# The first layer's last three modulations: VectorE products with row sums in place of plain TensorE matmuls

## The chip, the cores and the metric

The kernel runs on one core of a Trainium2 chip. The metric is the device time of one execution in microseconds (us). Engines are named as the profile names them: PE is TensorE (PEld its weight loads), DVE is VectorE, ACT is ScalarE, POOL is GpSimd, and SP is SyncE, whose queue issues nearly all DMAs of this kernel.

## The reference, cut to what matters

Two layers of a diffusion backbone over 256 context and 256 latent tokens of width 1024. Each layer is a half-step SwiGLU, four token mixers side by side on one normalised input (an S5 recurrence, a latent attention MLA, an HGRN2 recurrence and a grouped attention GQA), merged by gates, and a second half-step SwiGLU. Every sub-layer is modulated by shift, scale and gate vectors that come from the conditioning:

```
mod_lat = (jax.nn.silu(c) @ w_ada[layer] + b_ada[layer]).reshape(b, 1, N_MOD, D_MODEL)
mod_ctx = (jax.nn.silu(c_ctx) @ w_ada[layer] + b_ada[layer]).reshape(1, 1, N_MOD, D_MODEL)
```

So there are nine modulations a layer, each a product of two vectors (latent and context) with a 1024 x 1024 matrix of weights, 4 MB. Numbers 6, 7 and 8 are the shift, scale and gate of the second SwiGLU; they are needed only at the end of the mixing stage and after it.

## The kernel before

The activations stand transposed, 128 channels to a partition block and 512 tokens along the row. Every large product is written as three fp32r matmuls on a high and a low part of both operands (`mm3`, lines 345 to 347). A weight piece is 128 x 1024: `piece` (line 323) loads it through the SP queue into one of three buffers (`wraw`, tile `raw`), ACT casts the high part (L317, `whi`) and DVE subtracts for the low part (L318, `wlo`).

The program is `begin`, `ffn(0,0)`, `mix(0)`, `ffn(0,1)`, `ffn(1,0)`, `mix(1)`, `ffn(1,1)`. In `mix`, generators stand for the pieces of work. `lane` (line 1649) steps through tracks of attention or recurrence work, and after each step `fill` adds a share of projection and merge matmuls ("fillers", tiles `pj`, `pk`, `br`) that keep PE busy, and `next(self.slow)` takes one step of a slow side job, here the modulations. The slow job starts with the GQA track (line 1722) and has 24 steps. In layer 0 the second plan entry, `h|GM`, runs the second HGRN half (`h`) beside GQA and then MLA (`G`, `M`).

The text is recorded in this order, and a scheduler then gives each engine a fixed sequence of its own, which the engine works through in order; between engines only semaphores decide. The attention's unit (`attend`, line 836) is a chain over three engines: score matmul `s` (PE, L841), row maximum and its negation (DVE, L843 and L844), exponential `e` (ACT, L846), reciprocal and scaling (DVE, L847 and L848), transposes `pt` (PE, L853), a copy `p` (DVE L858 or ACT L856), and the product with the values `od` (PE, L868). The HGRN half has similar chains: `ckd`, `cqd` and `cx` between DVE (L1088, L1090, L1127 to L1133) and ACT, `ckt`, `cst`, `clv` and `cdg` on PE.

There are two ways to compute a modulation. `ada_pe` (line 434) does it on PE: for each of 8 pieces of 128 input rows (tile `araw`, in the same three `wraw` buffers) four plain fp32 matmuls with the two vectors as a 32-column stationary operand, into one PSUM bank of tag `f` that is held for all 8 steps, then one DVE copy (`adaev`, L448) and two PE transposes (`adat`, L451):

```
for q in range(4):
    nc.tensor.matmul(ps[32 * q : 32 * q + 32, :256], self.cS[:, kb], raw[:, 256 * q : 256 * q + 256], ...)
```

`ada` (line 401) does it on DVE from a transposed copy of the weights (`w_adaT`, output channels on partitions): for each half of the inputs (`kh`) it loads the two vectors spread over all partitions (`cr`, L411), applies Silu on ACT (L412), and for each of 4 pieces a modulation does four products with a row sum (L424), each over 128 x 512. It is the way the other modulations are done (0,2 to 0,5 beside the first SwiGLU; all of layer 1 beside SwiGLUs):

```
w = raw[:, 512 * i : 512 * i + 512]
for v in range(2):
    nc.vector.scalar_tensor_tensor(w if v else junk, w, 1.0, S[v], op0=ALU.mult, op1=ALU.mult,
                                   accum_out=t[:, 2 * op + i, v : v + 1])
```

`modulation` (line 457) adds the bias and the norm weights in either case.

Of the kernel before, what the change touches and what calls it, by code (L numbers as in the profile page):

```python
# [27 lines left out]
ALL_T = (0, NTOK)  # L28
# [158 lines left out]
class Kern:  # L187
# [295 lines left out]
    def begin(self, lag=1, first=1, spread=3, early=0):  # L483
# [4 lines left out]
        m = self.mod[0][:2] = [self.cpool.tile([P, KB, 2], F32, name=f"mod0_{j}") for j in range(2)]  # L488
        H, ws, banks = self.new_h(), [], []

# [42 lines left out]
        for t in range(KB + lag):  # L533
# [7 lines left out]
            for half in hv:  # L541
                p, q = half[1]
                self.pre_block(0, 0, ob, H, half, rs[:, p:q])
            if first <= ob < first + 4:
# [3 lines left out]
            for i, w in enumerate(ws):  # L548
                for kb in range(ob + 1) if i == ob - first else (ob,):
                    c = slice(kb * P, kb * P + P)  # L550
                    self.mm3(banks[i], (w[0][:, c], w[1][:, c]), H[kb], kb == 0, kb == KB - 1)
            mark, tc.cur_priority = tc.cur_priority, now
        tc.cur_priority = mark
        return H, banks

    def pre_block(self, l, s, kb, H, half, rs):

        nc = self.nc
        v, (a, b) = half
        sh, sc = self.mod[l][3 * s], self.mod[l][3 * s + 1]  # L560
        hh, hl = H[kb]
        t = self.u("ht")
        nc.vector.scalar_tensor_tensor(
            t[:, a:b], self.x[kb][:, a:b], sc[:, kb, v : v + 1], rs, op0=ALU.mult, op1=ALU.mult)
        nc.scalar.activation(hh[:, a:b], t[:, a:b], AF.Identity, bias=sh[:, kb, v : v + 1])  # L565
        nc.vector.scalar_tensor_tensor(
            hl[:, a:b], t[:, a:b], sh[:, kb, v : v + 1], hh[:, a:b].bitcast(F32), op0=ALU.add, op1=ALU.subtract)
# [1198 lines left out]
    def run(self):  # L1766
        nc = self.nc
        self.setup()
        self.opt = [
            dict(plan=('H', 'h|GM', 'S'), rates=(1.5, 0.4, 1, 1, 1), share=0.75, pk='f', pv='a', pq='a', vtt='a', us='a', s1='f', sD='f', cap=18, gap=1),  # L1770
            dict(plan=('H', 'h', 'G', 'M', 'S'), rates=(1.7, 1.3, 1.5, 1.5, 0.8), share=0, pk='a', pv='a', pq='a', vtt='f', us='a', s1='f', sD='f', cap=12, gap=2),
        ]

        H, banks = self.begin()
        self.gpre += self.vectors("norm_pre", 24, [1])
        self.gpost = self.vectors("norm_post", 24, range(DEPTH))
        self.mvec = self.vectors("mvec", 8, range(DEPTH))
        self.beside = [[self.ada(0, range(2, 6), False), 0.6, 0], [self.behind(self.s5_tables(0)), 0.6, 0]]
        W = self.A["ffn"]
        head = lambda l: [self.A["win"][l, i] for i in FIRST]  # L1780
        H = self.ffn(0, 0, ALL_T, H, (0, 1), head(0), banks)
        self.finish()
        self.lower_bounds()
        H = self.mix(0, ALL_T, H, (0, 2), (x for j in range(6, 9) for x in self.ada_pe(0, j)), [W[1, i] for i in range(self.start)])
        self.beside = [[self.behind(self.s5_tables(1)), 0.6, 0], [self.behind(self.ada(1, range(3), False)), 0.6, 0]]
        H = self.ffn(0, 1, ALL_T, H, (1, 0), [W[2, i] for i in range(self.start)])
        self.finish()
        self.beside = [[self.behind(self.ada(1, range(3, 9))), 0.9, 0]]
        H = self.ffn(1, 0, ALL_T, H, (1, 1), head(1))
        self.finish()  # L1790
        H = self.mix(1, LAT_T, H, (1, 2), iter(()), [W[3, i] for i in range(4)])
        self.ffn(1, 1, LAT_T, H, None)
        for kb in range(KB):
            nc.sync.dma_start(self.out[kb * P : (kb + 1) * P, :], self.x[kb][:, NCTX:])
# [23 lines left out]
```

## Time and profile before

| | |
|---|---|
| median of 3 runs | 2426.26 us (2425.04 to 2430.54) |
| the profiled execution: its own time | 2430.84 us |
| its span, first to last instruction | 2429.1 us, mean granted TensorE clock 0.972 |
| PE busy | 2278.5 us, 94% of the span |
| PEld busy | 1923.3 us, 79% |
| DVE busy | 1641.2 us, 68% |
| ACT busy | 902.7 us, 37% |
| POOL busy | 166.4 us, 7% |
| DMA | 326.84 MB, mean 135 GB/s |

Times in the rows are in us from the start of the span unless marked ns. A busy time is the time in which at least one instruction of the engine runs. An instruction's duration and the spacing to the next one differ, since neighbours overlap. What an engine does on the average of the span says little here: the change touches one stretch, and what bounds that stretch has to be read there.

### The profile page before, as it was taken

How to read it: one execution, taken by the hardware profiler on the slowest of the kernel's cores; microseconds unless marked ns; L12 is line 12 of the kernel's file. 1: busy time of each engine (PE TensorE's matmuls, PEld its weight loads, DVE VectorE, ACT ScalarE, POOL GpSimd, SP SyncE). 2: the span in 40 equal slices, each digit the busy share in tenths (PEclk: the TensorE clock that was granted, in tenths of full speed). 3: DMA queues.
4: the chain of work that ended last, by engine and by line, in shares of the span. 5: the costliest groups of instructions: out<-in, count | busy, mean ns of one | idle time of the engine just before them, and what ended most of it. 6: DMA issues, size and time to landing. Idle time of an engine off the chain costs nothing.

```text
span 2429.1 us, 39327 instructions
## 1 busy us (share of the span) xinstructions
PE 2278.5 (94%) x15428; PEld 1923.3 (79%) x15428; DVE 1641.2 (68%) x3929; ACT 902.7 (37%) x1551; POOL 166.4 (7%) x144
## 2 busy tenths in 40 slices
PE   7969989999999999988799999999998999998997
PEld 4757878987667777887677898888898887898997
DVE  5876566766565565799665558868757787678554
ACT  3313323363443323442222233323234664345443
POOL 0093000000000000006510000000000000000000
PEclk9989999999999999999899999999998999998999
DMA  7526454232441242233454423656542332354663
GB/s 237 180 90 183 155 170 156 73 94 77 132 161 41 86 150 83 79 122 120 149 166 158 135 86 117 204 177 196 173 139 81 109 109 69 122 187 134 186 184 114
DMA packets 111226, 326.84 MB, mean 135 GB/s; under 512 B 16256, under 2 KB 23168, under 8 KB 111040
## 3 DMA queue, kind: packets, MB, share of 16 engines
q1 hardware_dynamic: 109024, 320.65, 42.8%
q10 hardware_dynamic: 2016, 3.67, 0.5%
q8 instruction: 121, 1.98, 0.3%
q14 instruction: 65, 0.53, 0.1%
HBM read 311.20 MB, written 15.17 MB: 134 GB/s over the span
## 4 chain that ended last, share of the span: by engine, by line
PE 73%; DVE 14%; DMA 6%; ACT 3%; issue 2%; POOL 2%; SPq 0%; DVEq 0%; ACTq 0%; POOLq 0%
PE h L345 8%; PE h L347 8%; PE h L346 8%; PE y L345 5%; PE y L347 5%; PE y L346 5%; PE pj L345 5%; PE pj L347 5%; PE pj L346 5%; DMA araw<-in_w_adaT_dram 3%; DVE wlo L318 3%; DVE aj L424 2%; DMA raw<-in_ffn_dram 2%; PE s L841 2%; DVE araw L424 1%
## 5 line engine op out<-in xcount | busy, mean ns | idle before, releaser
L317 ACT CAST whi<-raw 128x1024 fp32r<-128x1024 f32 x402 | 421.1, 1050 | 843.0 <-DMA raw<-in_ffn_dram 308.8
L318 DVE TENSOR_TENSOR wlo<-raw,whi 128x1024 fp32r<-128x1024 f32 x402 | 499.5, 1245 | 302.9 <-ACT whi L317 300.3
L347 PE MATMUL h<-hh,wlo 128*128 128x512 f32 (+1 forms) x1472 | 529.8, 361 | 22.1 <-DVE wlo L318 22.1
L345 PE MATMUL h<-hh,whi 128*128 128x512 f32 (+1 forms) x1472 | 531.2, 362 | 16.8 <-DVE gf L686 11.2
L346 PE MATMUL h<-hl,whi 128*128 128x512 f32 (+1 forms) x1472 | 528.3, 360 | 0.0
L347 PEld LDWEIGHTS h<-hh,wlo 128*128 128x128 f32 x1472 | 283.4, 193 | 67.7 <-DVE wlo L318 24.7
L345 PEld LDWEIGHTS h<-hh,whi 128*128 128x128 f32 x1472 | 284.1, 193 | 62.0 <-issue 12.1
L346 PEld LDWEIGHTS h<-hl,whi 128*128 128x128 f32 x1472 | 284.0, 193 | 39.2
L345 PE MATMUL y<-gh,whi 128*128 128x256 f32 (+1 forms) x902 | 290.3, 322 | 2.6 <-ACT t L685 2.6
L347 PE MATMUL y<-gh,wlo 128*128 128x256 f32 (+1 forms) x902 | 290.8, 323 | 0.0
L346 PE MATMUL y<-gl,whi 128*128 128x256 f32 (+1 forms) x902 | 290.5, 322 | 0.0
L345 PE MATMUL pj<-hh,whi 128*128 128x256 f32 (+1 forms) x800 | 276.5, 348 | 3.3 <-ACT hh L565 2.7
L347 PE MATMUL pj<-hh,wlo 128*128 128x256 f32 (+1 forms) x800 | 274.5, 345 | 3.5 <-DVE wlo L318 3.5
L346 PE MATMUL pj<-hl,whi 128*128 128x256 f32 (+1 forms) x800 | 275.4, 346 | 0.0
L345 PEld LDWEIGHTS y<-gh,whi 128*128 128x128 f32 x902 | 171.7, 190 | 15.7 <-ACT t L685 2.8
L346 PEld LDWEIGHTS y<-gl,whi 128*128 128x128 f32 x902 | 171.7, 190 | 13.0
L347 PEld LDWEIGHTS y<-gh,wlo 128*128 128x128 f32 x902 | 171.7, 190 | 12.8
L345 PEld LDWEIGHTS pj<-hh,whi 128*128 128x128 f32 x800 | 154.1, 194 | 23.6 <-issue 5.2
L347 PEld LDWEIGHTS pj<-hh,wlo 128*128 128x128 f32 x800 | 153.9, 193 | 23.6 <-DVE wlo L318 4.8
L346 PEld LDWEIGHTS pj<-hl,whi 128*128 128x128 f32 x800 | 154.2, 193 | 18.4 <-issue 3.9
L424 DVE SCALAR_TENSOR_TENSOR aj<-araw,cr 128x512 f32<-128x512 f32 x112 | 89.8, 802 | 81.8 <-DMA araw<-in_w_adaT_dram 80.1
L687 ACT CAST gh<-gf 128x512 fp32r<-128x512 f32 (+1 forms) x88 | 49.8, 565 | 161.4 <-DVE gf L686 160.0
(391 smaller groups left out, 3188.3 us busy)
## 6 DMA issues: line engine op xcount, KB each, us to landing
raw<-in_ffn_dram SPq DMA_DIRECT2D x267, 512.0 KB, 3.8
araw<-in_w_adaT_dram SPq DMA_DIRECT2D x104, 512.0 KB, 4.1
raw<-in_win_dram SPq DMA_DIRECT2D x102, 512.0 KB, 3.7
araw<-in_w_ada_dram SPq DMA_DIRECT2D x24, 512.0 KB, 4.0
raw<-in_wout_dram SPq DMA_DIRECT2D x17, 512.0 KB, 3.5
raw<-in_wbr_dram SPq DMA_DIRECT2D x16, 512.0 KB, 3.7
araw<-in_w_ada_dram SPq DMA_DIRECT2D x22, 256.0 KB, 5.9
s5G<-s5g SPq DMA_DIRECT2D x16, 256.0 KB, 4.5
```

Source lines behind the costliest of these rows:

```text
L317: self.nc.scalar.copy(hi, src)
L318: self.nc.vector.tensor_tensor(lo, src, hi.bitcast(F32), op=ALU.subtract)
L345: mm(ps, wh, xh, start=start, stop=False, skip_group_check=True)
L346: mm(ps, wh, xl, start=False, stop=False, skip_group_check=True)
L347: mm(ps, wl, xh, start=False, stop=stop, skip_group_check=True)
L424: nc.vector.scalar_tensor_tensor(w if v else junk, w, 1.0, S[v], op0=ALU.mult, op1=ALU.mult, accum_out=t[:, 2 * op + i, v : v + 1])
L687: nc.scalar.copy(gh[:, a:b], gf[:, a:b])
L841: nc.tensor.matmul(s[:, :w], q[:, j * P : (j + 1) * P], k[:, :w], start=True, stop=True)
```

## The change

In `mix(0)` the slow side job is another generator:

```diff
-        H = self.mix(0, ALL_T, H, (0, 2), (x for j in range(6, 9) for x in self.ada_pe(0, j)), [W[1, i] for i in range(self.start)])
+        H = self.mix(0, ALL_T, H, (0, 2), self.ada(0, range(6, 9), False), [W[1, i] for i in range(self.start)])
```

With `banks` False the Silu results stay in SBUF (`cr` is overwritten in place). Both generators have 24 steps and load 24 pieces of 512 KB through the SP queue. `ada_pe` finishes one modulation after another; `ada` does the first half of the inputs for all three, then the second half, so that modulation 6 is ready after step 16.

The fixed sequences of three engines, at three places. In the names, the part behind the underscore is a running number.

DVE, one GQA unit in the middle of the stretch, from its row maximum to its scaled exponentials. Before:

```order
L843 TENSOR_REDUCE m_5716<-s_5714 128x1
L1107 SCALAR_TENSOR_TENSOR cst_5576<-cst_5576,et_5638,cst_5693 128x64
L844 TENSOR_SCALAR m_5716<-m_5716 128x1
L318 TENSOR_TENSOR wlo_5766<-raw_5763,whi_5765 128x1024
L1107 SCALAR_TENSOR_TENSOR cst_5576<-cst_5576,et_5638,cst_5693 128x64
L847 RECIPROCAL m_5716<-m_5716 128x1
L1127 TENSOR_TENSOR cx_5735<-cw_5591 128x512
L848 TENSOR_SCALAR e_5719<-e_5719,m_5716 128x256
```

The same unit in the changed kernel, with a few rows ahead of it:

```order
L1107 SCALAR_TENSOR_TENSOR cst_5576<-cst_5576,et_5647,cst_5702 128x64
L424 SCALAR_TENSOR_TENSOR araw_5712,mod_6_5631<-araw_5712,cr_5637 128x512
L424 SCALAR_TENSOR_TENSOR aj_5640,mod_6_5631<-araw_5712,cr_5634 128x512
L843 TENSOR_REDUCE m_5725<-s_5723 128x1
L424 SCALAR_TENSOR_TENSOR araw_5712,mod_6_5631<-araw_5712,cr_5637 128x512
L844 TENSOR_SCALAR m_5725<-m_5725 128x1
L424 SCALAR_TENSOR_TENSOR aj_5640,mod_7_5632<-araw_5732,cr_5634 128x512
L424 SCALAR_TENSOR_TENSOR araw_5732,mod_7_5632<-araw_5732,cr_5637 128x512
L424 SCALAR_TENSOR_TENSOR aj_5640,mod_7_5632<-araw_5732,cr_5634 128x512
L847 RECIPROCAL m_5725<-m_5725 128x1
L1127 TENSOR_TENSOR cx_5744<-cw_5591 128x512
L848 TENSOR_SCALAR e_5728<-e_5728,m_5725 128x256
```

The products stand between the unit's own steps; the next units look alike, until all 96 are done.

PE, the scores of the unit before that and what follows. Before:

```order
L853 MATMUL pt_5658<-cst,e_5601 128x128 x2
L841 MATMUL s_5663<-dq_5077,dq_4801 128x256
L442 MATMUL adaps_5631<-araw_5703,cS 32x256 x3
L347 MATMUL pj_5613<-hh_3591,wlo_5610 128x512
L345 MATMUL pj_5613<-hh_3593,whi_5609 128x512
L442 MATMUL adaps_5631<-araw_5723,cS 32x256
L1095 MATMUL ckt_5687<-cst,ckd_5640 128x128 x2
L442 MATMUL adaps_5631<-araw_5723,cS 32x256 x3
L346 MATMUL pj_5613<-hl_3594,whi_5609 128x512
L347 MATMUL pj_5613<-hh_3593,wlo_5610 128x512
L1095 MATMUL ckt_5687<-cst,ckd_5640 128x128
L1100 MATMUL cst_5693<-vc_4311,ckt_5688 64x64 x2
```

In the changed kernel:

```order
L347 MATMUL pj_5613<-hh_3593,wlo_5610 128x512
L853 MATMUL pt_5667<-cst,e_5601 128x128 x2
L841 MATMUL s_5672<-dq_5077,dq_4801 128x256
L1095 MATMUL ckt_5696<-cst,ckd_5649 128x128 x3
L1100 MATMUL cst_5702<-vc_4311,ckt_5697 64x64 x2
L853 MATMUL pt_5718<-cst,e_5677 128x128 x2
L841 MATMUL s_5723<-dq_5077,dq_4801 128x256
```

The modulation matmuls are gone and nothing has moved into their place. From the first of these score matmuls to the twelfth, PE has 120 projection matmuls before and 110 in the changed kernel; four of the ten stand ahead of the first one now, the rest behind the twelfth.

ACT, ahead of the first of these units' exponentials. Before:

```order
L1086 ACTIVATE et_5638<-cw_5591 128x1
L1087 ACTIVATE ckd_5640<-cw_5591 128x128
L1086 ACTIVATE et_5638<-cw_5591 128x1
L1087 ACTIVATE ckd_5640<-cw_5591 128x128
L1086 ACTIVATE et_5638<-cw_5591 128x1
L1087 ACTIVATE ckd_5640<-cw_5591 128x128
L1089 ACTIVATE cqd_5639<-cw_5591 128x512
L846 ACTIVATE e_5668,m_5665<-s_5663,m_5665 128x256
```

In the changed kernel:

```order
L1086 ACTIVATE et_5647<-cw_5591 128x1 x3
L412 ACT_TABLE_LOAD
L412 ACTIVATE cr_5634<-cr_5634 128x512
L412 ACTIVATE cr_5637<-cr_5637 128x512
L1087 ACT_TABLE_LOAD
L1087 ACTIVATE ckd_5649<-cw_5591 128x128 x3
L1089 ACTIVATE cqd_5648<-cw_5591 128x512
L846 ACTIVATE e_5677,m_5674<-s_5672,m_5674 128x256
```

Two Silu and two table loads stand ahead of the exponentials now. The same four instructions stand a second time in the middle of the stretch, for the second half of the inputs.

## Rows read from the trace of the kernel before

**Rows 1.** The page, part 1: busy time (share of span) and instructions by engine.

```profile
PE 2278.5 (94%) x15428; PEld 1923.3 (79%) x15428; DVE 1641.2 (68%) x3929; ACT 902.7 (37%) x1551; POOL 166.4 (7%) x144
```

**Rows 2.** Busy time by stretch: PE, PEld, DVE, ACT, POOL (instructions), clock, DMA share, GB/s.

```profile
629.87:715.10 85.23, 81.26 (x801) 47.99 (x801) 53.41 (x157) 35.06 (x82) 1.36 (x3) 0.96 0.52 168
720.00:1000.00 280.00, 274.20 (x1836) 213.24 (x1835) 164.72 (x309) 97.25 (x175) 0.45 (x4) 0.99 0.29 90
```

**Rows 3.** Chain of work that ended last, 600 to 760 us, by line.

```profile
by line: PE pj L345 15.9%; PE pj L347 14.8%; PE pj L346 14.0%; PE adaps L442 9.7%; PE s L841 8.0%; PE od L868 5.2%; PE cdg L1174 4.7%; PE pt L853 4.5%; PE hs L787 3.4%; PE oc L1192 2.9%; DMA araw<-in_w_ada_dram 2.5%; PE hb L810 2.1%; PE oc 
```

**Rows 4.** Line 442, all its matmuls (duration ns min/median/max, first and last start).

```profile
L442 PE MATMUL adaps<-araw,cS x192: 379/379/636, 623.7 to 707.3; 128*32 128x256 f32 x192
```

**Rows 5.** PE in order of time: start, us, what.

```profile
626.99 0.64 PE L442 MATMUL adaps<-araw,cS 128*32 128x256 f32 x8
627.56 0.50 PE L345 MATMUL pj<-hh,whi 128*128 128x512 f32 x1
627.90 0.40 PE L346 MATMUL pj<-hl,whi 128*128 128x512 f32 x1
```

**Rows 6.** Line 424 where it runs before (columns as in rows 4).

```profile
L424 DVE SCALAR_TENSOR_TENSOR aj<-araw,cr x112: 673/687/1553, 77.5 to 1314.1; 128x512 f32<-128x512 f32 x112
L424 DVE DVE_READ_ACCUMULATOR aj<-araw,cr x112: 71/82/86, 78.1 to 1314.8; 128x1 f32 x112
```

**Rows 7.** Line 424 alone, 1480 to 1800 us: DVE busy, clock, DMA share, GB/s.

```profile
1480.00:1800.00 320.00, 128.87 (x384) 1.00 0.58 179
```

**Rows 8.** DVE in order of time: first and last row maximum of the twelve units.

```profile
629.87 0.42 DVE L843 TENSOR_REDUCE m<-s 128x1 f32<-128x256 f32 x1 [1.22 <-PE s L841]
715.10 0.68 DVE L843 TENSOR_REDUCE m<-s 128x1 f32<-128x512 f32 x1
```

**Rows 9.** DVE groups, 629.87 to 715.10: busy us, mean ns, idle before, releaser.

```profile
L318 DVE TENSOR_TENSOR wlo<-raw,whi 128x1024 fp32r<-128x1024 f32 x6 | 7.3, 1220 | 0.7 <-ACT whi L317 0.7
L843 DVE TENSOR_REDUCE m<-s 128x1 f32<-128x256 f32 x7 | 3.0, 424 | 7.7 <-PE s L841 7.7
L843 DVE TENSOR_REDUCE m<-s 128x1 f32<-128x512 f32 x4 | 2.8, 692 | 3.5 <-PE s L841 3.5
...
L847 DVE RECIPROCAL m<-m 128x1 f32<-128x1 f32 x11 | 1.8, 160 | 3.0 <-ACT e L846 2.8
...
L960 DVE SCALAR_TENSOR_TENSOR bs<-bc,mvec,hb 128x512 f32<-128x512 f32 x2 | 1.5, 748 | 2.1 <-PE hb L810 2.1
...
L1090 DVE TENSOR_TENSOR cqd<-cqd,cq 128x512 f32<-128x512 f32 x2 | 1.4, 684 | 0.0
L448 DVE COPY adaev<-adaps 128x256 f32<-128x256 f32 x3 | 1.3, 420 | 3.6 <-PE adaps L442 3.6
...
L296 DVE SCALAR_TENSOR_TENSOR ry<-rt,ry 128x4 f32<-128x4 f32 x6 | 1.0, 163 | 0.2
...
L464 DVE TENSOR_TENSOR mod<-adat,bada 128x16 f32<-128x16 f32 x3 | 0.5, 169 | 0.2 <-PE adat L451 0.2
```

**Rows 10.** ACT groups of the whole span: Silu, and one table load.

```profile
L412 ACT ACTIVATE cr<-cr 128x512 f32<-128x512 f32 x8 | 5.0, 630 | 4.3 <-DMA cr<-in_cR_dram 4.1
...
L846 ACT ACT_TABLE_LOAD x1 | 1.3, 1283 | 0.0
```

**Rows 11.** DMA issues of the whole span: count, KB each, median us to landing.

```profile
araw<-in_w_adaT_dram SPq DMA_DIRECT2D x104, 512.0 KB, 4.1
...
araw<-in_w_ada_dram SPq DMA_DIRECT2D x24, 512.0 KB, 4.0
...
cr<-in_cR_dram SPq DMA_DIRECT2D x12, 256.0 KB, 4.9
```

**Rows 12.** Busy time by stretch, columns as in rows 2: DVE-bound, start of this mixing stage.

```profile
455.00:470.00 15.00, 11.50 (x84) 10.98 (x83) 15.00 (x40) 7.98 (x17) 0.53 (x1) 0.86 0.09 29
465.00:470.00 5.00, 2.87 (x16) 2.79 (x16) 5.00 (x11) 1.01 (x2) 0.53 (x1) 0.57 0.27 83
470.00:475.00 5.00, 5.00 (x35) 5.00 (x35) 3.01 (x13) 1.42 (x2) 0.00 (x0) 0.75 0.85 255
```

## The prediction, made before the changed kernel had run

> **What bounds the kernel now.** I read the page first. PE is busy 94% of the span and DVE 68% [rows 1], so work that leaves PE looks like gain and work that goes to DVE looks covered. These are averages over stages, so the next view is the busy time in the stretch that the change touches. The old modulation matmuls run from 623.7 to 707.3 us [rows 4], and in the fixed sequences their work and the new products stand beside twelve units of grouped attention, whose first and last row maximum start at 629.87 and 715.10 us [rows 8]. In these 85.23 us PE is busy 81.26 us and DVE 53.41 us [rows 2]: PE is the bound here too, and DVE has 31.8 us of idle time. The chain of waits says the same: nearly all of it is PE, with the modulation matmuls at 9.7% of the 160 us shown [rows 3]. The DVE groups say what the idle time is made of: mostly waits for score matmuls (7.7 and 3.5 us), for the copy of the modulation bank (3.6) and for exponentials (2.8) [rows 9]. The reader is to see that DVE's idle time is short waits inside chains that PE later depends on, and that 31.8 us of it is all there is.
>
> **What is removed.** PE loses 24 groups of matmuls, one for each weight piece. One group takes 0.57 us of PE's time, from its start at 626.99 to the next start at 627.56 [rows 5]; 24 of them make 13.7 us. Three pairs of transposes and DVE's three bank copies go with them, and with the copies 3.6 us of DVE's waits [rows 9]. As long as PE is the bound this is worth about 14 us; once it isn't, nothing. The loads stay 24 pieces of 512 KB in the same three buffers and land in 4.1 instead of 4.0 us [rows 11]; no price. The bank of tag f is free for the whole stretch now, but the sequence of PE shows no filler that uses this to come forward by more than four matmuls.
>
> **What is added.** DVE gets 96 products with a row sum. The same instruction runs elsewhere in this kernel: 687 ns, and 82 ns to read out the sum, partly under the product [rows 6]. Counted as busy time in a stretch where 192 of them run, it is 128.87 / 192 = 0.671 us each [rows 7], so 96 take 64.4 us. That is twice what DVE has idle between the twelve units. All 96 stand between the first and the last row maximum in DVE's new sequence, five to fifteen of them from one row maximum to the next, so none can wait for a quieter time; and what PE has between its twelve score matmuls isn't more than before but ten projection matmuls less. The stretch therefore cannot end before DVE is through.
>
> **The sum for the stretch.** DVE's old work there is 53.41 us. Of it go three bank copies of 0.42 us, and the scheduler has moved two low parts of weights (1.22 each), two norm products (0.75) and nine small steps of a root (0.16) behind the last unit [rows 9]; with the small modulation steps that is 6.6 us. So 46.8 + 64.4 = 111.2 us of DVE work for a stretch that took 85.2 us. The lower end is DVE without idle time: +26 us. The nearest row for that is 455 to 470 us, where DVE is the bound and is busy 15.0 of 15 us [rows 12]. The upper end keeps all of today's 31.8 us idle: 143 us, +58. Between them I look at which waits survive. Waits for scores and exponentials shrink, because products stand between the unit's steps; the waits for the bank copies are gone. New ones come at two places where ACT applies Silu to the spread vectors: a table load of 1.28 us, 0.63 us for each vector, and a table load back [rows 10]. At the first place the vectors have long landed and DVE loses about 1 us. At the second, the vectors' load stands in SP's queue behind a weight piece that waits for a buffer, and lands 4.9 us after issue [rows 11]; DVE has some 2 us of other work, a row maximum (0.69 [rows 9]) with its exponential and scaling, so I put 3 us, and ACT's exponentials queue behind the same Silu. With 8 us for the rest I take 12 us of idle time: a stretch of 123 us, **+38 us**. That is nearer to the busy end, since the row of 455 to 470 us is the same engine in the same stage with a queue that is always full.
>
> **Behind the stretch.** Ten projection matmuls fewer stand in it, four of which run ahead of it; six at 0.34 us [rows 5] are 2 us that PE does later. The 6.6 us that DVE does later fit there: from 720 to 1000 us it is idle 115 of 280 us [rows 2]. Can the loss be caught up? Only where PE idles later in this stage, and in the same 280 us that is 5.8 us [rows 2]. I take 2 us of that, which cancels the 2 us; the whole 5.8 us goes into the low end (+20).
>
> The profiled execution took 2430.84 us and would take 2469; the median of the runs shown is 4.6 us lower, so the forecast is 2426.3 + 38 = **2464 us**.
>
> **A rule against the change.** A product with a row sum takes 687 ns [rows 6], a plain product of the same 128 x 512 size 684 ns [rows 9]: the sum costs no rate. The Trainium skill (Vector Engine (DVE) Microarchitecture Reference, "Points that are easy to get wrong") says of this instruction's operand layout that two non-bf16 sources halve its throughput. Both sources here are fp32, so by it one would expect about twice the plain product, 96 x 0.68 = 65 us more. This case's trace doesn't agree, with 687 beside 684 ns; the sum goes by the trace.
>
> **Rivals.** (1) *PE's clock falls.* When DVE held the queue from 465 to 470 us, PE was busy 2.87 of 5 us and the granted clock was 0.57, near the lower level of 1.2 GHz; in the next 5 us it was still 0.75 [rows 12]. In the new stretch PE would be busy about 67 of 123 us (81.26 less 13.7), a share like that one. At the lower level throughout, 67 us become 134 and PE and DVE would take turns as the bound: 134 plus the 4 us that PE idles today is 138 us, +53, and with up to 7 us of waits between the two +60: 2479 to 2486 us. Against it: the products stand between chain steps, so PE's gaps are short, and fillers run in most of them. The Trainium skill (TensorE: Matmul & The Clock Gate, "What's actually happening") describes the low clock as the default that activity releases; the rows agree in direction, and how often it happens here no row shows. (2) *Faster.* PE stays the bound, because the products fall into DVE's waits and weights still arrive in time: minus 13.7 us of matmuls, 2412 us. It decides whether DVE's work per unit stays under PE's, some 71 us in the stretch without the modulation matmuls. For it speaks that DVE is idle 31.8 us there and 115 of the 280 us behind it [rows 2]; against it that the fixed sequence keeps all 96 between the twelve units, 111 us against 71. (3) *No difference.* PE's 14 us outweigh most of the waits for DVE; that needs a stretch under 90 us, less than DVE's bare work. (4) *Products at half rate*, by the page's rule: 96 x 0.68 = 65 us on top, 2529 us; the 687 ns of today speak against it.
>
> **How the numbers follow.** The main case, DVE as the bound of the stretch, gets 0.74; the clock 0.16; faster 0.05; no difference 0.04; half rate 0.01. Less than 0.2% (4.9 us) can't be told from no change in a measurement of this kernel. The range runs from +20 (no idle time, all of PE's later idle time used) to +60: **2446 to 2486 us**. It takes in the main case and nearly all of the clock's. Faster 0.05, same 0.04, slower 0.91.
>
> **What would show it.** In the changed profile the distance from the first to the last of these twelve row maxima is the test: 111 to 143 us, 123 expected, instead of 85.2. DVE should be busy about 90% in it, PE some 55%, and PE's longest waits should be for DVE (scaled exponentials, `cx`, `ckd`). The 96 products should take 64 us of DVE. From the last unit on, the distance to the end of this mixing stage should be as before within some 5 us. I am wrong if the stretch stays under 100 us, if a granted clock well below 0.9 is what fills it, or if DVE idles in it for weight loads, which I price at nothing because a buffer comes free some three pieces ahead of its use.

## The result, and the profile after

The changed kernel takes 2467.53 us (median of 4 runs, 2462.99 to 2474.86) beside 2426.86 us of the kernel before: a ratio of 1.0164, 95% interval 1.0143 to 1.0185. That is +41 us, 3.5 us above the forecast of 2464. The profiled execution took 2470.79 us, its span is 2468.9 us. The page's first part, which answers to [rows 1], shows DVE's added work (1641.2 to 1696.9 us) and next to no change of PE's sum:

```profile
PE 2279.0 (92%) x15230; PEld 1930.5 (78%) x15230; DVE 1696.9 (69%) x4121; ACT 909.8 (37%) x1559; POOL 166.0 (7%) x144
```

The twelve units answer to [rows 8]; DVE in order of time, around the first row maximum with the first product, and at the last one:

```profile
628.20 0.42 DVE L843 TENSOR_REDUCE m<-s 128x1 f32<-128x256 f32 x1 [1.16 <-PE s L841]
...
629.20 0.69 DVE L424 SCALAR_TENSOR_TENSOR aj<-araw,cr 128x512 f32<-128x512 f32 x1 [0.38 <-ACT cr L412]
...
748.31 0.42 DVE L858 COPY p<-pt 128x256 f32<-128x256 f32 x1
748.65 0.68 DVE L424 SCALAR_TENSOR_TENSOR araw<-araw,cr 128x512 f32<-128x512 f32 x1
749.26 0.08 DVE L424 DVE_READ_ACCUMULATOR araw<-araw,cr 128x1 f32 x1
749.39 0.69 DVE L843 TENSOR_REDUCE m<-s 128x1 f32<-128x512 f32 x1
```

From 628.20 to 749.39 are 121.19 us, where the kernel before took 85.23. Busy time in this stretch and from it to the first output matmul of the stage (columns as in [rows 2]: length, PE, PEld, DVE, ACT, POOL, granted clock, DMA share, GB/s), and the second of the two before:

```profile
628.20:749.39 121.19, 78.81 (x604) 51.18 (x606) 104.33 (x333) 41.66 (x91) 1.27 (x3) 0.70 0.41 124
749.39:1028.60 279.21, 272.77 (x1834) 212.67 (x1835) 164.36 (x321) 94.39 (x169) 0.45 (x4) 0.98 0.30 93
```

```profile
715.10:989.10 274.00, 268.20 (x1813) 208.40 (x1813) 160.63 (x306) 93.30 (x169) 0.45 (x4) 0.99 0.29 91
```

DVE is busy 86% of the stretch, and PE, busy 95% before, 65%, at a granted clock of 0.70 instead of 0.96. The first maximum comes 1.7 us earlier than before; 1.4 us of this stand ahead of the first projection matmul already (460.2 instead of 461.6 us), where the change does nothing. The 279.21 us behind the stretch were 274.0 before (715.10 to 989.1). So the way to the output matmuls is -1.7 + 36.0 + 5.2 = +39.5 us, and the whole span +39.8.

The groups of DVE in the stretch (columns as in [rows 9]):

```profile
L424 DVE SCALAR_TENSOR_TENSOR araw<-araw,cr 128x512 f32<-128x512 f32 x48 | 32.9, 685 | 0.5
L424 DVE SCALAR_TENSOR_TENSOR aj<-araw,cr 128x512 f32<-128x512 f32 x48 | 32.8, 684 | 3.2 <-ACT cr L412 3.2
...
L843 DVE TENSOR_REDUCE m<-s 128x1 f32<-128x256 f32 x7 | 2.9, 421 | 5.2 <-PE s L841 5.2
L843 DVE TENSOR_REDUCE m<-s 128x1 f32<-128x512 f32 x4 | 2.8, 689 | 0.6 <-PE s L841 0.5
```

A product takes 684 or 685 ns here, as elsewhere before [rows 6]. DVE's waits for scores fell from 11.2 us [rows 9] to 5.7: products stand in their place. The waits of the stretch, by who waits for whom (us in all, times, longest), and the first of them before:

```profile
ACT e L846 <- DVE m L844: 20.6, 8, 6.1
...
ACT whi L317 <- DMA raw<-in_win_dram: 12.9, 5, 4.4
...
PE cdg L1174 <- DVE cx L1133: 11.4, 2, 9.1
...
PE pj L345 <- ACT whi L317: 8.8, 2, 5.3
...
DVE hv L792 <- PE hs L787: 4.8, 2, 3.7
```

```profile
ACT e L846 <- DVE m L844: 12.3, 8, 3.9
```

The exponentials wait longer for DVE's maxima, PE waits for DVE's `cx` (up to 9.1 us in a row), and projections wait for weights that came late. The last wait isn't in the forecast at all. What I had priced at nothing was another, DVE idle for the products' weights, and that didn't occur: 5.7 us of DVE's 16.9 us of idle time are waits for scores, 4.8 for the sums of the norms (`hs`), 3.2 for Silu, and no wait for a load shows.

### The profile page after: what moved, and what is told of

The parts are those of the page before. It is cut to its first block, busy times and chain, and to the rows that moved or that the text cites. A ratio compares the mean times of both kernels' runs of the same rounds, so it can differ in the third digit from the quotient of the medians.

```text
span 2468.9 us, 39135 instructions
## 1 busy us (share of the span) xinstructions
PE 2279.0 (92%) x15230; PEld 1930.5 (78%) x15230; DVE 1696.9 (69%) x4121; ACT 909.8 (37%) x1559; POOL 166.0 (7%) x144
## 4 chain that ended last, share of the span: by engine, by line
PE 70%; DVE 17%; DMA 6%; ACT 3%; issue 2%; POOL 1%; SPq 0%; DVEq 0%; ACTq 0%; POOLq 0%
PE h L345 8%; PE h L347 8%; PE h L346 7%; PE y L345 5%; PE y L347 5%; PE y L346 5%; PE pj L345 5%; PE pj L347 5%; PE pj L346 5%; DVE wlo L318 3%; DMA araw<-in_w_adaT_dram 3%; DVE aj L424 3%; DVE araw L424 2%; PE s L841 2%; ACT whi L317 2%
## 5 line engine op out<-in xcount | busy, mean ns | idle before, releaser
L345 PE MATMUL h<-hh,whi 128*128 128x512 f32 (+1 forms) x1472 | 530.9, 362 | 17.7 <-DVE gf L686 11.9
L345 PEld LDWEIGHTS h<-hh,whi 128*128 128x128 f32 x1472 | 283.7, 193 | 63.4 <-issue 12.1
L345 PE MATMUL y<-gh,whi 128*128 128x256 f32 (+1 forms) x902 | 290.3, 322 | 2.6 <-ACT t L685 2.6
L345 PE MATMUL pj<-hh,whi 128*128 128x256 f32 (+1 forms) x800 | 279.7, 352 | 12.0 <-ACT whi L317 8.8
L345 PEld LDWEIGHTS y<-gh,whi 128*128 128x128 f32 x902 | 171.7, 190 | 15.7 <-ACT t L685 2.8
L345 PEld LDWEIGHTS pj<-hh,whi 128*128 128x128 f32 x800 | 155.7, 196 | 33.5 <-ACT whi L317 9.3
L424 DVE SCALAR_TENSOR_TENSOR aj<-araw,cr 128x512 f32<-128x512 f32 x160 | 122.6, 766 | 85.5 <-DMA araw<-in_w_adaT_dram 80.1
L424 DVE SCALAR_TENSOR_TENSOR araw<-araw,cr 128x512 f32<-128x512 f32 x160 | 122.1, 764 | 2.6
```

What stands on the lines that cost most here:

```text
L345: mm(ps, wh, xh, start=start, stop=False, skip_group_check=True)
```

## The experiments

Each experiment is an edit of the changed kernel. "The stretch" is from the first to the last of the twelve row maxima (lines shift by a few where code was added). The table is read from the windows of each trace; the ratio is to the kernel before on the same chip.

| kernel | DVE busy | PE busy, clock | stretch | time, us | ratio, 95% interval |
|---|---|---|---|---|---|
| before | 53.4 | 81.3, 0.96 | 85.2 | 2426.9 | |
| changed | 104.3 | 78.8, 0.70 | 121.2 | 2467.5 | 1.0164 [1.0143, 1.0185] |
| e1, + 4 matmuls a step | 105.5 | 87.2, 0.77 | 123.4 | 2470.4 | 1.0177 [1.0159, 1.0194] |
| e12, + 8 matmuls a step | 103.8 | 95.7, 0.84 | 119.7 | 2466.7 | 1.0168 [1.0147, 1.0189] |
| e2, no modulations | 52.2 | 73.6, 0.82 | 86.1 | 2419.6 | 0.9960 [0.9946, 0.9975] |
| e5, short products | 71.1 | 81.3, 0.77 | 101.9 | 2437.6 | 1.0045 [1.0029, 1.0060] |
| e3, half the products | 83.2 | 81.3, 0.71 | 111.1 | 2452.3 | 1.0100 [1.0078, 1.0121] |
| e9, e3 + 4 matmuls a step | 83.0 | 93.4, 0.78 | 114.4 | 2454.3 | 1.0123 [1.0095, 1.0150] |
| e6, e3 + 8 matmuls a step | 83.3 | 98.0, 0.92 | 106.6 | 2443.9 | 1.0073 [1.0047, 1.0100] |

**e1: the products, and PE's work as well.** `with_pe` passes the steps of `ada` on and adds four matmuls a step over a constant; with `range(8)`, the second four into the other half of the bank, it is e12.

```diff
-        H = self.mix(0, ALL_T, H, (0, 2), self.ada(0, range(6, 9), False), [W[1, i] for i in range(self.start)])
+        H = self.mix(0, ALL_T, H, (0, 2), self.with_pe(self.ada(0, range(6, 9), False)), [W[1, i] for i in range(self.start)])
+    def with_pe(self, gen):
+        for n, x in enumerate(gen):
...
+            for q in range(4):
+                self.nc.tensor.matmul(ps[32 * q : 32 * q + 32, :256], self.cS[:, n % 8], self.cst[:, :256], ...)
+            yield x
```

> The changed kernel, and beside its products the PE work of the removed matmuls: 96 plain fp32 matmuls of the old size, over a constant tile instead of the loaded weights, so that they wait for nothing; their result is used nowhere. Theory D (DVE's queue is the bound of the stretch, PE only follows): PE has some 42 us idle among the twelve units, the 14 to 27 us of matmuls fit there, and the time stays within 8 us of the changed kernel (2460 to 2476 us). Theory C (the matmuls run at half clock and PE is the bound): either the clock stays low and the time rises to 2481 to 2495 us, or the added activity keeps the clock high and the time falls to some 2445 us or less.

PE did 8.4 us more in the stretch, and the kernel took 2470.4 us, within the spread of the changed kernel and of theory D's range. In the changed kernel PE has room; what the change took from it is worth nothing there.

**e2: no modulations.** The generator `no_ada` fills the three vectors with a constant instead.

```diff
+            self.nc.vector.memset(m, 0.5)
```

> The three modulations are left out: a constant stands in for modulations 6 to 8 of the first layer, and neither the matmuls, the products nor their loads run. It prices the old matmuls alone. If PE is the bound of the old stretch, as the prediction took it, this is 10 to 18 us faster than before: 2409 to 2417 us, with the stretch of twelve units at 67 to 75 us. If the chains of the units are the bound and the old matmuls fell into their waits, it is within 5 us of before.

2419.6 us, 9 us under the 2428.95 of the kernel before in the same comparison: a little less than the 10 to 18 expected with PE as the bound, and more than the 5 with the chains. The stretch, which the first theory put at 67 to 75 us, did not get shorter:

```profile
623.43:709.48 86.05, 73.56 (x635) 50.00 (x637) 52.24 (x149) 33.91 (x80) 1.36 (x3) 0.82 0.14 41
```

With the modulation matmuls gone, the twelve units take as long as before (86.05 beside 85.23). PE is busy 8 us less and idles 12.5 instead of 4.0 us, at a clock of 0.82, and DVE isn't full either. Two causes remain, and no run parts them. The units may have a length of their own by then, the chain from score to weighted values; or the lower clock takes back what the removed matmuls gave, since the chain's own matmuls take longer. Those of the scores before and in e2:

```profile
L841 PE MATMUL s<-dq,dq 64*128 64x256 f32 (+1 forms) x22 | 9.8, 525 | 0.0
```

```profile
L849 PE MATMUL s<-dq,dq 64*128 64x256 f32 (+1 forms) x22 | 11.5, 610 | 0.2 <-ACT cS L1159 0.2
```

The first maximum comes 6.4 us earlier than before, but this isn't the price of the matmuls: 6.2 us of it stand ahead of the first projection matmul (455.4 instead of 461.6 us), where nothing was changed. The projection matmuls (L345) before and in e2, with the first and last start:

```profile
L345 PE MATMUL pj<-hh,whi x800: 274/388/581, 461.6 to 2177.2; 128*128 128x256 f32 x81, 128*128 128x512 f32 x79
```

```profile
L345 PE MATMUL pj<-hh,whi x800: 274/388/583, 455.4 to 2163.7; 128*128 128x256 f32 x81, 128*128 128x512 f32 x79
```

In the traces of the twelve kernels with the same program ahead of it, the first of these matmuls starts between 455.2 and 462.9 us, so differences of a few us between two whole kernels can come from there. What e2 gains in this stage stands behind the stretch: from 709.48 us to the first output matmul at 976.8 it takes 267.3 instead of 274.0 us.

**e3: half of the products.** Only the context sums (`v` = 0) are made, as `self.whole` is False during this stage; loads, Silu and steps are all there.

```diff
-                        for v in range(2):
+                        for v in range(2 if self.whole else 1):
```

> The changed kernel with half of the products: only those with the context vector, 48 instead of 96; the latent sums stay zero, the loads stay. Theory D: DVE's work among the twelve units falls from 104 to some 72 us, and with 17 us of waits the stretch takes some 85 to 92 us: 2424 to 2436 us, that is nearly the whole loss gone, not half. If the loss is a price per product, half of it stays: 2447 us. Theory C: the matmuls are still gone from PE and the clock still falls: over 2447 us.

2452.3 us: theory D, DVE as a bound that leaves its idle time to the products, expected 2424 to 2436 and failed; the time is nearest to the two others, a price per product (2447) and theory C (over 2447). DVE's work is 83.2 us and not the 72 expected, which is part of the miss. The window, and two of PE's groups:

```profile
628.48:739.59 111.11, 81.28 (x620) 53.23 (x622) 83.24 (x254) 43.41 (x93) 1.36 (x3) 0.71 0.52 159
```

```profile
L845 PE MATMUL s<-dq,dq 64*128 64x256 f32 (+1 forms) x22 | 12.8, 673 | 0.2 <-DVE cC L1183 0.2
...
L1178 PE MATMUL cdg<-cx 64*32 64x32 f32 x192 | 2.4, 214 | 7.7 <-DVE cx L1137 7.7
```

DVE idles 28 of 111 us and PE 30, and still the stretch is 25 us longer than without modulations, for 31 us of added DVE work. So DVE needn't be full for a product to cost. The second half costs less: from e3 to the changed kernel DVE's work grows by 21.1 us and the stretch by 10.1, 0.48 us for each, while DVE's idle time falls from 27.9 to 16.9 us. The score matmuls average 673 ns where they took 525 before, so the low clock is a rival here; e6 and e9 are about it.

**e5: the products' length, or what comes with them?** 96 products, but over 64 columns.

```diff
+                            c = slice(0, 512 if self.whole else 64)
...
+                                (w if v else junk)[:, c], w[:, c], 1.0, S[v][:, c], op0=ALU.mult, op1=ALU.mult,
```

> All 96 products stay in the twelve units, with the same loads, Silu and reads of the sum, but each runs over 128x64 instead of 128x512 (seven eighths of every sum is left out). Theory 'length of the products': what the stretch loses is their time on DVE, which in this kernel's in-order queue is paid almost in full; with some 15 us instead of 64 the stretch takes 92 to 100 us and the kernel 2425 to 2436. Theory 'all that comes with them' (the loads of the spread vectors, Silu and its table loads, weights that wait for a buffer): these are unchanged, so at least 20 of the 41 us stay and it takes 2447 or more.

2437.6 us, between the two, near the theory of the length. The window and the two groups of short products:

```profile
631.17:733.08 101.91, 81.33 (x647) 53.89 (x647) 71.13 (x353) 44.90 (x95) 1.36 (x3) 0.77 0.55 174
```

```profile
L426 DVE SCALAR_TENSOR_TENSOR araw<-araw,cr 128x64 f32<-128x64 f32 x48 | 10.5, 222 | 0.9
L426 DVE SCALAR_TENSOR_TENSOR aj<-araw,cr 128x64 f32<-128x64 f32 x48 | 10.5, 219 | 3.9 <-DMA araw<-in_w_adaT_dram 2.2 <-ACT cr L413 1.6
```

An eighth of the columns takes a third of the time (220 ns beside 685), which I had put at about 160. DVE's work is 18.9 us above e2's and the stretch 15.9 us longer: 0.84 us for each. In e3 it is 25.0 / 31.0 = 0.81, in the changed kernel 35.1 / 52.1 = 0.67. The price follows the added DVE time: the loads and Silu are the same in e3, e5 and the changed kernel. They aren't shown to be free, since no run has them without products; a straight line through e3 and e5, or through e5 and the changed kernel, leaves 2 to 5 us for them (an estimate).

**e6 and e9: the clock, with half of the products.** `with_pe` around e3, with eight and four matmuls a step.

> The 48 products of the half version, and beside each of the 24 steps eight matmuls of 32x256 over a constant, twice the PE work of the old modulations in number of matmuls. The half version took 2452 with a stretch of 111 us, in which neither DVE (83 us) nor PE (81 us at a granted clock of 0.71) was full. Theory 'clock': PE's low clock stretches its chain steps by some 14 us; with PE kept busier the clock rises to 0.8 or more and the time falls to 2438 to 2447. Theory 'in-order queue': the products stand ahead of the chain's DVE steps, the stretch stays at 108 to 118 us whatever the clock, and the kernel takes 2449 to 2460.

> As the half version with PE work beside it, but with four matmuls of 32x256 a step, the number that the old modulations had, so that PE is not filled by them. With eight the stretch fell from 111 to 106.6 us while the granted clock rose from 0.71 to 0.92, but PE was then busy 98 us. Theory 'clock': the clock is what the half version loses to; with about 87 us of PE work at 0.8 or more the stretch takes 98 to 104 us and the kernel less than 2444. Theory 'in-order queue': the products delay the chain by themselves; the stretch stays at 105 to 112 us and the kernel at 2444 to 2455.

The windows, and the score matmuls; e6:

```profile
626.01:732.62 106.61, 98.01 (x992) 58.76 (x991) 83.29 (x254) 45.12 (x95) 1.30 (x3) 0.92 0.53 166
```

```profile
L857 PE MATMUL s<-dq,dq 64*128 64x256 f32 (+1 forms) x22 | 10.3, 551 | 0.1
```

e9:

```profile
628.21:742.60 114.39, 93.42 (x784) 56.28 (x785) 82.97 (x254) 43.14 (x93) 1.36 (x3) 0.78 0.50 155
```

```profile
L857 PE MATMUL s<-dq,dq 64*128 64x256 f32 (+1 forms) x22 | 12.8, 673 | 0.0
```

With eight a step, which make PE's busy time in the stretch 16.7 us longer, the kernel is faster: 2443.9 (2442.99 to 2445.19) beside 2452.3 us (2447.43 to 2458.93), as theory 'clock' expected. The two ran on different chips; beside the kernel before on the same chip they lose 17.6 and 23.3 us, and the intervals of the ratios overlap at their ends. From the first projection matmul to the first output matmul the traces take 545.4 and 552.6 us. The clock rose to 0.92 and the scores fell to 551 ns. With four, the score matmuls didn't get shorter (673 ns), and nothing was gained: the time is in the range of the in-order theory, the stretch in neither. As the scores kept their length, e9 doesn't speak against the clock. How much of the remaining 20 us is products ahead of chain steps and how much clock stays open: the matmuls that raise it also fill PE to 98 of 106.6 us, and 132 projection matmuls stand in e6's stretch instead of 114, so the clock isn't all that differs.

**e12: the clock, with all products.**

> The changed kernel with eight matmuls of 32x256 over a constant beside each of the 24 steps (e1 had four). With 48 products, eight a step brought the score matmuls from 673 to 551 ns and the kernel down by 8 us, though they are 25 us of PE's time; four a step did nothing. With all 96 products: theory 'DVE is the bound of the stretch' has 104 us of DVE work whatever the clock, so the stretch stays at 118 to 126 us and the kernel at 2463 to 2478. Theory 'clock' has PE's slow chain steps as part of the 17 us that DVE idles; the stretch falls below 116 us and the kernel below 2460.

```profile
626.93:746.66 119.73, 95.68 (x960) 55.41 (x961) 103.79 (x333) 41.77 (x91) 1.30 (x3) 0.84 0.40 126
```

```profile
L853 PE MATMUL s<-dq,dq 64*128 64x256 f32 (+1 forms) x22 | 12.2, 641 | 0.2 <-DVE cC L1191 0.2
```

2466.7 us, as the changed kernel. The clock rises from 0.70 to 0.84 and the score matmuls fall from 706 to 641 ns, and the stretch shortens by 1.5 us only: DVE has 104 us of work in it either way. This fits DVE as the bound and the low clock as a consequence, as the first theory expected. It doesn't prove it: the added matmuls make PE's busy time 16.9 us longer as well, and what they delay could hide what the clock gave.

**e8: lower priority for the products** (`self.behind(self.ada(...))` in the call of `mix`).

> The products get a lower priority in the scheduler; DVE's fixed sequence then has 12 of the 96 after the twelfth row maximum and fewer ahead of the first steps, but still 4 to 14 between two maxima. Theory 'in-order queue': nearly the same work stands in the same chains, 2458 to 2472. Theory 'it is the priority': products give way to chain steps, DVE's idle time takes them, and it takes less than 2450.

```profile
623.04:740.72 117.68, 80.12 (x602) 52.38 (x604) 99.83 (x318) 39.45 (x89) 1.25 (x3) 0.67 0.41 119
```

2463.0 us, ratio 1.0151 [1.0116, 1.0187]: as expected by the in-order theory. A priority doesn't help where nearly the same products stand between the same steps.

**e4: the same products beside the first SwiGLU.**

```diff
-        self.beside = [[self.ada(0, range(2, 6), False), 0.6, 0], [self.behind(self.s5_tables(0)), 0.6, 0]]
+        self.beside = [[self.ada(0, range(2, 9), False), 1.0, 0], [self.behind(self.s5_tables(0)), 0.6, 0]]
```

> The same 96 products, beside the first SwiGLU instead of the attention: the side job of that stage makes modulations 2 to 8, one step for each weight piece, and the mixing stage has no side job. From 60 to 460 us DVE was idle 126 of 400 us before, twice what is added, but PE idled 36 us there too, so DVE is near its limit in parts of it. Theory D (where DVE has room the products cost little): the mixing stage gains the 14 us of the matmuls and the SwiGLU loses 0 to 30 us: 2410 to 2442 us, well under the changed kernel. If 64 us of DVE work cost their price wherever they stand: 2450 us or more.

2452.2 us, ratio 1.0095 [1.0080, 1.0110]. The twelve units are as without modulations, clock and all:

```profile
655.37:741.43 86.06, 73.57 (x635) 50.13 (x637) 52.26 (x149) 33.91 (x80) 1.36 (x3) 0.82 0.14 41
```

The first projection matmul starts at 487.5 us instead of 455.4 in e2: the whole price, 32 us for 64 us of products, is paid in the SwiGLU (the medians say 32.6; 0.5 us for each us of products). Expected was less, and by the words of the expectation this is the other theory, that products cost their price wherever they stand; but it is 15 us less than beside the twelve units by the medians (20 by the start of the output matmuls, 1008.2 beside 1028.6 us).

**e7 and e11: the products later.** `self.slow = more` moves from the grouped to the latent attention (`mla`); e11 also ties the first three loads to Silu.

```diff
+                    if l == 0 and 6 in js and n == 0 and op < 3:
+                        nc.scalar.copy(raw[:, :1], S[1][:, :1])
```

> The products start with the latent attention instead of with the grouped attention: the first twelve units have none, about half stand in later units between 785 and 845 us, the rest behind them. DVE is idle more there (in the kernel before 66 of 125 us from 775 to 900). Theory 'place': a product costs only where it stands in a chain that PE has nothing to cover; PE is 98% busy there, so most are free: 2425 to 2440, and the twelve units take about 86 us as without modulations. Theory 'every product costs about 0.4 us wherever it stands': 2455 or more.

> The late version, with one element of each of the first three modulation pieces written by ACT after Silu, so that their loads cannot take the three weight buffers before the spread vectors are there. In the late version three pieces were issued at 651 to 715 us and held all three buffers until the first products at 779, and from 690 to 780 us one projection weight was loaded, where the kernel before loads nine. Theory 'blocked buffers': the 83 us that this version loses were mostly that; 2430 to 2470. Theory 'the products themselves in this place': 2495 or more.

2509.0 us, ratio 1.0342 [1.0311, 1.0373], and 2512.1, 1.0352 [1.0316, 1.0388]: a clear miss, twice. One number that e7's expectation rested on was misread: DVE is idle 48.6 of the 125 us from 775 to 900 us in the kernel before (busy 76.42), not 66. In e7 the twelve units take 86.08 us as expected. But then PE loses work before the first product runs (779 us); the windows:

```profile
624.43:710.51 86.08, 73.59 (x635) 50.14 (x637) 52.24 (x149) 33.92 (x80) 1.36 (x3) 0.82 0.14 41
710.51:778.84 68.33, 56.01 (x561) 43.99 (x561) 32.84 (x92) 23.53 (x52) 0.00 (x0) 0.85 0.07 21
```

SP's queue of e11 in order of time (DMA issues) has no projection weight between 648 and 791 us, where the kernel before issues twelve:

```profile
631.25 16.78 SPq L326 DMA_DIRECT2D raw<-in_win_dram  x4
661.50 0.33 SPq L933 DMA_DIRECT2D mw<-in_w_ukv_dram  x1
743.13 5.01 SPq L933 DMA_DIRECT2D mw<-in_w_uq_dram  x2
754.61 3.33 SPq L411 DMA_DIRECT2D cr<-in_cR_dram  x2
778.51 10.24 SPq L422 DMA_DIRECT2D araw<-in_w_adaT_dram  x5
791.45 0.33 SPq L326 DMA_DIRECT2D raw<-in_win_dram  x1
```

The tie freed the three buffers, and the gap stayed, so my theory of blocked buffers falls. The projection weights stand behind the loads of the spread vectors and of the modulation pieces in SP's order now; PE lacks fillers (56.0 of 68.3 us busy from 710.51 us on in e7, where the kernel before has 67.9 of 68.1 from 715.10 on; 51 projection matmuls there, 126 before), and the work piles up at the end of the stage. That the place in the queue alone does it wasn't tried.

**e10: own buffers and the POOL queue for the products' weights.**

```diff
+                            w = self.wada.tile([P, 512], F32, tag="ada", name=self.nm("araw"))
+                            nc.gpsimd.dma_start(w, self.A["w_adaT"][l, kh, j, op][:, 512 * i : 512 * i + 512])
```

> The changed kernel, but the weights of the products come through the POOL queue into two buffers of 128x512 of their own (48 loads of 256 KB; two of the 33 general slots pay for them), so that neither the SP queue nor the three weight buffers of the projections wait for a product. Theory 'DVE is the bound of the stretch': PE's 9 us of waits for projection weights go, DVE's 104 us of work do not; 116 to 124 us from the first to the last of the twelve maxima, 2458 to 2472. Theory 'weights': the projections are late because products hold their buffers; the stretch falls below 112 us and the kernel below 2455.

2501.75 us, ratio 1.0320 [1.0292, 1.0348]; neither theory was tested. Waits from 620 to 760 us:

```profile
PE cdg L1181 <- DVE cx L1140: 20.9, 3, 8.1
...
DVE aj L431 <- DMA araw<-in_w_adaT_dram: 12.1, 17, 1.8
```

With two small buffers DVE waits for loads, and its queue with it (the stretch takes 146.6 us). Away from the products time is lost as well: the first projection matmul starts at 470.0 instead of 460.2 us, and from the first output matmul of this stage to the last of layer 1's it is 1233.0 us instead of 1217.9. The two general slots that pay for the buffers are the likely cause, but no run took them alone. Whether late projection weights cost anything beside a full DVE stays open.

## Why the prediction was right, and where it wasn't

- **DVE becomes the bound of the stretch:** right in the number, 121.2 us measured and 123 forecast. DVE is busy 104.3 us of them, so the stretch can't be shorter than that. In e1 and e12 PE's work and clock rise by much and the time stays.
- **The products:** 64.4 us forecast, and line 424 alone is busy 64.87 us there.
- **DVE's work in all:** 111 forecast, 104.3 measured. Outside the products that leaves 39.5 us, where 46.8 were counted. The sum added two busy times, but neighbours on DVE overlap when the queue is full: the copy at 748.31 ends at 748.73, the product behind it starts at 748.65. An estimate from these two rows, 96 times 0.08, is 8 us.
- **Idle time:** 12 forecast, 16.9 measured. Silu took 0.38 and 2.85 us (1 and 3 forecast), so the miss is in the 8 us "for the rest", which were 13.7: waits for scores (5.7) and for `hs` (4.8) above all. Waits for the products' weights were priced at nothing and were nothing. The errors of -7 and +5 nearly cancel, and the -2 that is left and the 1.7 us ahead of the stretch cover most of the 5.2 behind it: that 2464 lies so near is in part luck.
- **Behind the stretch:** I let 2 us of later fillers and 2 us of recovery cancel. It is 5.2 us longer, with 4.6 us more PE work (272.77 beside 268.20 us from 715.10 on): the fillers cost more than the 2 us, and nothing was recovered.
- **Rival 1, the clock:** its condition came true in part, its price did not. The granted clock fell to 0.70 on the mean, not to the lower level throughout, and PE is busy 78.8 us (65%) where I had 67 (55%). That the low clock fills the stretch, which I had named as a sign of being wrong, e12 makes unlikely, with the limit said there.
- **What the forecast would have got wrong with less work:** that products first use up DVE's idle time. e3 was expected by this rule, and with half of the products the stretch is already 25 us longer than in e2, of 35 us with all. The sum "work plus a few waits" held only because 96 products keep DVE nearly full (86%).
- **Rival 4, half rate:** no; 684 and 685 ns in the place itself.
- **The removed matmuls:** 13.7 us while PE is the bound, and PE was taken as the bound of the old stretch. e2 doesn't bear that out: without them the stretch is as long (86.05 us), and the kernel gains 9 us, elsewhere. Whether the chains or the lower clock keep the stretch up stays open.

No run beats the kernel before with its computation kept, and e2 bounds what any place for these modulations can bring: about 9 us (6 to 13 by its interval).

## What to carry to other kernels

Idle time of an engine inside chains that cross engines isn't free room: in these runs each us of work put between the steps cost 0.67 to 0.84 us on the mean, with a third of the added work as with all of it, and the idle share only gave the right sum once the engine was nearly full. A low granted clock in such a stretch can be cause or consequence. Matmuls over a constant are a test of it: they helped with half of the products (e6) and changed nothing where DVE was busy 86% (e12). It isn't a clean test, since they also take PE's time and move other work. When a side job moves, look at the order of the load queue first: in e7 and e11 its loads came to stand ahead of the projections' and PE ran short of work before any product had begun, though the order alone wasn't tried.

## What the runs showed that I had not expected

Added PE work can save time: with matmuls over a constant, busy 24.7 us, the half version was some 6 us faster beside the kernel before on the same chip (8 by the medians). In the changed kernel the granted clock stands at the lower of its two levels (0.50, 1.2 GHz) in stretches in which PE works on its chain for 6.5 of 8 us:

```profile
716.00:724.00 8.00, 6.54 (x30) 5.23 (x30) 3.55 (x11) 2.29 (x6) 0.00 (x0) 0.50 0.22 83
```

It had waited for DVE just before; PE in order of time:

```profile
711.51 2.08 PE L810 MATMUL hb<-cst,ry 128*128 128x128 f32 x8 [5.21 <-DVE ry L296]
714.86 4.17 PE L787 MATMUL hs<-cst,bs 128*128 128x1 f32 x16 [1.27 <-DVE bs L960]
```

The Trainium skill (TensorE: Matmul & The Clock Gate, "What's actually happening") describes the low clock as the default that activity releases; these rows show the low clock right after a wait of 5.21 us (0.50), and no release.
